# An encoder block on one core: where DRAM copies are issued, and which gate and up tiles use eight products

## The chip, the core and the metric

The kernel runs on one core of a Trainium2 chip. TensorE (PE) multiplies, VectorE (DVE), ScalarE (ACT) and GpSimd (POOL) do the elementwise work, and DMA engines move data between the device's memory (DRAM) and the on-chip memory, or within DRAM. Each engine has one queue and takes its instructions in order. DMAs are issued from the queues of SP (SyncE), ACT and POOL. The metric is the device time of one execution in microseconds (us); the median of several runs counts.

## What is computed

One layer, 512 tokens of width 1024, all in float32. From the reference, cut:

```python
h = rms_norm(x, norm_mix)
aq, ak, av, bq, bk, bv, ga, gb = split_cols(h @ w_in)
oa = gqa_attention(rope(rms_norm(aq)), rope(rms_norm(ak)), av)      # 8 heads of 64
ob = rms_norm(diff_attention(rope(bq), rope(bk), bv, lam), subln)   # 4 heads, two score maps each
y = sigmoid(ga) * (oa @ w_proj_a) + sigmoid(gb) * (ob @ w_proj_b)
x = x + y @ w_out
h = rms_norm(x, norm_ffn)
x = x + (silu(h @ w_gate) * (h @ w_up)) @ w_down                    # inner width 2816
return rms_norm(x, norm_final)
```

## The kernel before

**Precision.** Every float32 operand is split into a high part (a cast on ACT, `split_hi`) and a low part (the difference, on DVE, `split_lo`). A product is three matmuls, high by high, high by low, low by high (`mm3`, lines 92 to 94). `load_unit` (line 84) loads a weight unit of 128 x 1024 on SP's queue into a `raw` tile (three buffers) and splits it into `whi` and `wlo` (five buffers each).

**Stages.** First the projections of the first attention's heads (`group_a`) and of the first differential head (`group_b`). Then eight heads of the first attention (`attend_a`), with pieces of other work as fillers between heads. Then the four differential heads (`attend_b`), each woven with the projection of a later head or with gate columns (`gate_col`, products named gt). Then projections, output and the second norm. Last the channel mixer: gate and up in 22 tiles of 128 columns, and the down product.

**The differential heads.** For each of four token tiles `probs` makes two score maps (sc), their exponentials and reciprocals; POOL multiplies the first (p_b_..x, line 399), DVE combines both. The probabilities are transposed (ptp) and multiplied by the values (ob). Then the sums of squares pn go through POOL's power (rsb, line 112) into the matmuls pb (line 424).

**Sums of down weights.** The down product and gate and up use the seven products of a Strassen-like scheme. For the down product, sums and differences of weight blocks are formed in DRAM: tiles `td` of four kinds (td0 to td3), six pieces each. For each piece `tcopy` copies one block from `w_down` (line 453) and `tadd` adds a second one by an accumulating DMA (line 456). td1 adds td0's finished pieces, td3 those of td1. The list `tsums` runs through the kinds 0, 2, 1, 3; step k issues copy k and addition k - LAG, with LAG = 5. Copies and additions are all on POOL's queue. The steps stand in the four weaves with the differential heads, 8, 8, 7 and 6 of them.

**Gate and up.** Tiles 0 and 1 are computed as plain products by `ffn_in`, in two halves of 256 tokens: eight blocks of the inner width, twice (gate pg, up pu), three matmuls each. Tiles 2 to 21 use seven products of 256 columns (`g12`, `g5`, `g63`, `g7`, `g4`; q, p2 and r in the trace), 84 matmuls a tile. Their inputs come from `load_sums`: the raw unit, x (a load plus an accumulating load, lines 685 and 686), y (two DVE sums of x and raw, lines 694 and 695), each split; and from th and tl, sums of the hidden state, made on DVE after the norm with lowered priority. For tile 2 x and y take `raw` buffers (`early`).

**What sets the order.** The framework's scheduler orders each engine's queue by a simulated timeline; DMAs of `tsums` are kept in program order (`keep_in_program_order`). For every queue the order is fixed once the program is built.

Of the kernel before, what the change touches and what calls it, by code (L numbers as in the profile page):

```python
# [20 lines left out]
S = 512  # L21
# [5 lines left out]
NF = FF // P  # L27
# [2 lines left out]
LEFT_PAD = 48  # L30
RIGHT_PAD = 248
LATER = 400
LAG = 5


@with_exitstack
def kernel(
# [20 lines left out]
    nc = tc.nc  # L58
    v, a, g, pe = nc.vector, nc.scalar, nc.gpsimd, nc.tensor
# [312 lines left out]
    def attend_a(qT, kT, vt, fillers):  # L372
        for h in range(8):
            kv = h // 4
            if h >= 2:
                fillers[h - 2]()
            ps = []
            for tt in range(NT):
                nm = f"a{h}_{tt}"
                p_, r_ = probs(qT[h // 2][:, h % 2, :], kT[kv], tt, nm)  # L380
                g.tensor_scalar(out=p_, in0=p_, scalar1=r_, scalar2=1.0, op0=ALU.mult, op1=ALU.mult)  # L381
                ps.append(p_)
            av = ps_av.tile([P, S], F32, tag="av", name=f"oa_{h}")
            for kt in range(NT):
                ph, pl = transpose_p(ps, kt, f"a{h}_{kt}")
                pe.matmul(av, lhsT=vt[:, kt, kv, :], rhs=ph, start=kt == 0, stop=False)
                pe.matmul(av, lhsT=vt[:, kt, kv, :], rhs=pl, start=False, stop=kt == NT - 1)
            if h % 4 == 0:
                oA.append(u_tile(f"oA{kv}", F32))
            low = tmp.tile([HD, S], F32, tag="avt", bufs=1, name=f"low_{h}")  # L390
            a.copy(low, av[HD:P, :])
            v.tensor_tensor(out=oA[kv][HD * (h % 2):HD * (h % 2) + HD, h % 4 // 2, :], in0=av[0:HD, :], in1=low, op=ALU.add)
# [53 lines left out]
    tdram = [[dr.tile([P, 2, S], F32, name=f"td{i}_{p}") for p in range(NP)] for i in range(4)]  # L446
# [3 lines left out]
        return w_down[NU * j + 2 * p:NU * j + 2 * p + n, :, i * S:(i + 1) * S].rearrange("k p s -> p k s")  # L450

    def tcopy(i, p, src):
        return lambda: tc.keep_in_program_order(g.dma_start(tdram[i][p][:, :src.shape[1], :], src))

    def tadd(i, p, src):
        return lambda: tc.keep_in_program_order(g.dma_start(tdram[i][p][:, :src.shape[1], :], src, accum_op=ALU.add, max_dma_last_dim=4 * S))
# [7 lines left out]
    tsums = [tsum(i, p) for i in (0, 2, 1, 3) for p in range(NP)]  # L464
# [4 lines left out]
    def weave(*gens):  # L469
        gens = list(gens)  # L470
        while gens:
            for it in list(gens):
                if next(it, None) is None:
                    gens.remove(it)

    def steps(fs):
        for f in fs:
            f()
            yield True
# [8 lines left out]
        pe.matmul(pr[:, tt * P:(tt + 1) * P], lhsT=rstd[:, tt:tt + 1].to_broadcast([P, P]), rhs=ident, start=True, stop=True)  # L488
    a.copy(rstdB, pr)
    grp = [lambda: next(gen)]  # L490
    attend_a(*parts, grp * 3 + todo[:1] + grp + todo[1:2])
    weave(gen, steps(todo[2:4]))
    weave(attend_b(0, *nxt), group_b(2, nxt), steps(tsums[:8]))
    weave(attend_b(1, *nxt1), group_b(3, nxt1), steps(tsums[8:16]))
    weave(attend_b(2, *nxt), steps(todo[4:9]), steps(tsums[16:23]))
    weave(attend_b(3, *nxt1), steps(todo[9:13]), steps(tsums[23:]))
    for f in todo[13:]:
        f()
    attn.close()
# [151 lines left out]
    def bank(tag, nm, bufs=1):  # L651
        return ps_g.tile([P, S], F32, tag=tag, bufs=bufs, name=nm)
# [12 lines left out]
    def ffn_in(f, t0, t1, ug, uu):  # L665
        n = t1 - t0
        pg = bank("q", f"pg{f}_{t0}", 2)[:, :n]
        pu = bank("p2" if f else "r", f"pu{f}_{t0}")[:, :n]
        for acc, (hi, lo) in ((pg, ug), (pu, uu)):
            for kt in range(KT):  # L670
                c = slice(kt * P, (kt + 1) * P)
                mm3(acc, hi[:, c], lo[:, c], hh_[:, kt, t0:t1], hl_[:, kt, t0:t1], kt == 0, kt == KT - 1)
        t_ = (acts[f] if t0 else act_tile(f))[:, t0:t1]
        a.activation(t_, pg, AF.Sigmoid)
        v.tensor_tensor(out=t_, in0=pg, in1=t_, op=ALU.mult)
        v.tensor_tensor(out=t_, in0=pu, in1=t_, op=ALU.mult)
        if t0 == 0:
            act_parts(f)

    def load_sums(f):  # L680
        raw = wp.tile([P, UNIT], F32, tag="raw", bufs=3, name=f"raw_a{f}")
        nc.sync.dma_start(raw, w_gu[2 * f])
        early = f == 2
        x = wp.tile([P, UNIT], F32, tag="raw", bufs=3, name=f"x{f}") if early else tp_.tile([P, UNIT], F32, tag="x", bufs=3, name=f"x{f}")
        nc.sync.dma_start(x, w_x0[f])
        g.dma_start(x, w_x1[f], accum_op=ALU.add)  # L686
        r22 = tp_.tile([P, S], F32, tag="r22", bufs=3, name=f"r22_{f}")
        nc.sync.dma_start(r22, w_gu[2 * f + 1][:, S:])
        hi, lo = split_unit(raw, f"a{f}")
        w = wts[f] = {"11": (hi[:, :S], lo[:, :S]), "12": (hi[:, S:], lo[:, S:])}  # L690
        hi, lo = split_unit(x, f"x{f}")
        w["s1"], w["s3"] = (hi[:, :S], lo[:, :S]), (hi[:, S:], lo[:, S:])
        y = wp.tile([P, UNIT], F32, tag="raw", bufs=3, name=f"y{f}") if early else tp_.tile([P, UNIT], F32, tag="y", bufs=1, name=f"y{f}")
        v.tensor_tensor(out=y[:, :S], in0=x[:, :S], in1=raw[:, :S], op=ALU.add)
        v.tensor_tensor(out=y[:, S:], in0=y[:, :S], in1=raw[:, S:], op=ALU.add)
        hi, lo = split_unit(y, f"y{f}")
        w["s2"], w["s4"] = (hi[:, :S], lo[:, :S]), (hi[:, S:], lo[:, S:])
        h = sp_.tile([P, S], F32R, tag="h22", bufs=3, name=f"h22_{f}")
        l = sp_.tile([P, S], F32R, tag="l22", bufs=3, name=f"l22_{f}")
        split_hi(h, r22)  # L700
        split_lo(l, r22, h)
        w["22"] = (h, l)
# [17 lines left out]
    def g12(f):  # L720
        qb[f] = bank("q", f"q{f}", 2)[:, :H]
        p2 = bank("p2", f"p2_{f}")[:, :H]
        gprod(qb[f], f, "11", "11", True)
        gprod(p2, f, "12", "21", True, True)
        tg[f] = ft.tile([P, S], F32, tag="tg", name=f"tg{f}")
        a.copy(tg[f][:, :H], qb[f])
        v.tensor_tensor(out=tg[f][:, :H], in0=p2, in1=tg[f][:, :H], op=ALU.add)

    def g5(f):
        rb[f] = bank("r", f"r{f}")[:, :H]  # L730
        gprod(rb[f], f, "s1", "t1", True)
        p5c[f] = ft.tile([P, H], F32, tag="p5", name=f"p5_{f}")
        a.copy(p5c[f], rb[f])
# [78 lines left out]
    sums_a(0)  # L812
    p1 = [ps_d.tile([P, S], F32, tag="pd", name=f"p1_{b}") for b in range(2)]
    p2 = [ps_d.tile([P, S], F32, tag="pd", name=f"p2d_{b}") for b in range(2)]
    load_sums(2)
    g12(2)
    g5(2)
    for f in range(2, NF):
        if f + 1 < NF:
            load_sums(f + 1)  # L820
        g63(f)
        if f + 1 < NF:
            g12(f + 1)
        else:
            down0(NU - 2)
            pr_ = [bank("r", "pr_0"), bank("p2", "pr_1")]
        g7(f)
        if f + 1 < NF:
            g5(f + 1)
        else:  # L830
            product(0, 0, pr_, True, range(1))
        g4(f)
        if f % 2:
            sums_a(f // 2)
            if f + 1 < NF:
                down0(f // 2 - 1)
# [159 lines left out]
```

## Time and profile before

| | us |
|---|---|
| median of 3 runs | 761.25 (760.43 to 762.25) |
| profiled execution, whole time | 762.04 |
| profiled execution, span of the trace | 760.3 |
| TensorE busy in the span | 724.3 (95%) |
| VectorE busy | 553.0 (73%) |
| ScalarE busy | 423.8 (56%) |
| GpSimd busy | 193.9 (26%) |

Mean granted clock of TensorE 0.984 of full speed. All times in the trace are counted from the start of the span. A row of a timeline gives the start, the duration, the engine (SPq is the issuing queue of SP), the line, what is written and read without buffer numbers, and in brackets the idle time of the engine before it with what ended it. Durations of TensorE's matmuls overlap, so their pace is read from their starts.

### The profile page before, as it was taken

The page shows a single profiled execution, that of the slowest core. Times are in us where ns is not written, and L with a number is a line of the kernel's source. Part 1 is how long each engine was busy: PE and PEld are TensorE (multiplying, and loading weights), DVE is VectorE, ACT ScalarE, POOL GpSimd, SP SyncE. Part 2 cuts the span into 40 slices and gives each one's busy share as a digit, 9 for nine tenths or more (in the row PEclk, how much of TensorE's full clock was granted, in tenths as well). Part 3 has the DMA queues.
Part 4 walks back from the last instruction along what each step waited for, and adds up shares of the span by engine and source line. Part 5 has one row for each costly group of instructions (what it writes and reads, how often), then busy time and mean ns, then how long its engine had stood idle before and what let it go on. Part 6 is the DMA issues. An engine that isn't in the chain of part 4 may idle for free.

```text
span 760.3 us, 11984 instructions
## 1 busy us (share of the span) xinstructions
PE 724.3 (95%) x4407; PEld 651.0 (86%) x4407; DVE 553.0 (73%) x933; ACT 423.8 (56%) x765; POOL 193.9 (26%) x249
## 2 busy tenths in 40 slices
PE   5899999999999699899999999999999999999996
PEld 5789987789987588688888988999999999988885
DVE  5788698769876255458436779978887888877785
ACT  6356698867666366423226536555545555546672
POOL 3656443225774413010000021221221211110002
PEclk9899999999999889999999999999999999999999
DMA  8222212014999987514421289887777774459972
GB/s 316 82 65 75 57 45 81 8 41 137 274 300 282 298 193 156 187 52 137 139 83 48 64 251 293 243 225 236 218 208 224 200 194 158 146 172 332 320 270 110
DMA packets 46394, 131.52 MB, mean 173 GB/s; under 512 B 5664, under 2 KB 6560, under 8 KB 46336
## 3 DMA queue, kind: packets, MB, share of 16 engines
q1 hardware_dynamic: 29008, 84.55, 32.5%
q0 software_dynamic: 14736, 40.77, 23.3%
q10 hardware_dynamic: 2592, 5.45, 2.1%
q8 instruction: 34, 0.56, 0.3%
q14 instruction: 24, 0.20, 0.1%
HBM read 121.44 MB, written 32.37 MB: 202 GB/s over the span
## 4 chain that ended last, share of the span: by engine, by line
PE 75%; DMA 12%; DVE 5%; issue 3%; ACT 2%; POOL 2%; POOLq 0%; SPq 0%; ACTq 0%; DVEq 0%
DMA td<-in_w_down_dram 5%; PE q L92 5%; PE q L94 5%; PE q L93 5%; PE p L92 4%; PE p L93 4%; PE p L94 4%; DMA x<-in_w_x_dram 3%; PE r L94 2%; PE r L93 2%; PE r L92 2%; PE gt L92 2%; PE gt L93 2%; DMA td<-td 2%; PE gt L94 2%
## 5 line engine op out<-in xcount | busy, mean ns | idle before, releaser
L686 POOL DMA_DIRECT2D x<-in_w_x_dram x20 | 17.9, 894 | 130.2 <-DMA x<-in_w_x_dram 43.8
L93 PE MATMUL gt<-xgl,whi_g 128*128 128x512 f32 x128 | 51.0, 399 | 0.0
L92 PE MATMUL gt<-xgh,whi_g 128*128 128x512 f32 x128 | 51.0, 398 | 0.0
L94 PE MATMUL gt<-xgh,wlo_g 128*128 128x512 f32 x128 | 50.7, 396 | 0.0
L93 PE MATMUL acc_b<-wlo_b,xgh 128*128 128x384 f32 x128 | 43.6, 340 | 0.0
L92 PE MATMUL acc_b<-whi_b,xgh 128*128 128x384 f32 x128 | 43.4, 339 | 0.0
L94 PE MATMUL acc_b<-whi_b,xgl 128*128 128x384 f32 x128 | 43.4, 339 | 0.0
L763 POOL DMA_DIRECT2D sd<-s x44 | 28.8, 670 | 55.3 <-DVE s L760 25.3
L381 POOL TENSOR_SCALAR p_a<-p_a,r_a 128x512 f32<-128x512 f32 x32 | 23.7, 741 | 53.5 <-DVE r_a L359 46.0
L72 ACT CAST whi_y<-y 128x1024 fp32r<-128x1024 f32 x20 | 21.0, 1048 | 24.5 <-PE p2d L94 15.4
L79 DVE TENSOR_TENSOR wlo_y<-y,whi_y 128x1024 fp32r<-128x1024 f32 x20 | 24.4, 1222 | 10.0 <-ACT whi_y L72 10.0
L72 ACT CAST whi_a<-raw_a 128x1024 fp32r<-128x1024 f32 x20 | 21.0, 1048 | 16.6 <-issue 9.1
L79 DVE TENSOR_TENSOR wlo_t<-raw_t,whi_t 128x1024 fp32r<-128x1024 f32 (+1 forms) x24 | 27.0, 1130 | 3.2 <-ACT whi_t L72 3.0
L72 ACT CAST sh<-sr 128x512 fp32r<-128x512 f32 (+1 forms) x30 | 17.5, 583 | 21.1 <-PE p L93 8.0
L219 POOL TENSOR_TENSOR t_b<-z_b,csb 128x128 f32<-128x128 f32 x32 | 26.2, 947 | 11.7 <-ACT z_b L339 10.3
L94 PEld LDWEIGHTS gt<-xgh,wlo_g 128*128 128x128 f32 x128 | 24.4, 191 | 5.2
L93 PEld LDWEIGHTS gt<-xgl,whi_g 128*128 128x128 f32 x128 | 24.5, 191 | 4.9
L92 PEld LDWEIGHTS gt<-xgh,whi_g 128*128 128x128 f32 x128 | 24.3, 190 | 5.0
L92 PE MATMUL p<-whi_t,sh 128*128 128x512 f32 (+1 forms) x77 | 27.4, 360 | 1.0 <-DVE x L850 1.0
L357 ACT ACTIVATE p_a<-sc_a,nmax_a 128x512 f32<-128x512 f32 x32 | 22.4, 703 | 8.8 <-DVE nmax_a L354 7.9
L79 DVE TENSOR_TENSOR wlo_x<-x,whi_x 128x1024 fp32r<-128x1024 f32 x20 | 24.4, 1220 | 3.7 <-ACT whi_x L72 3.7
L93 PE MATMUL p<-wlo_t,sh 128*128 128x512 f32 (+1 forms) x77 | 26.9, 359 | 0.0
(391 smaller groups left out, 2815.1 us busy)
## 6 DMA issues: line engine op xcount, KB each, us to landing
td<-in_w_down_dram POOLq DMA_DIRECT2D x30, 512.0 KB, 16.9
raw_a<-in_w_gu_dram SPq DMA_DIRECT2D x20, 512.0 KB, 4.9
x<-in_w_x_dram SPq DMA_DIRECT2D x20, 512.0 KB, 4.9
x<-in_w_x_dram POOLq DMA_DIRECT2D x20, 512.0 KB, 6.7
raw_t<-td SPq DMA_DIRECT2D x20, 512.0 KB, 4.8
raw_g<-in_w_in_dram SPq DMA_DIRECT2D x16, 512.0 KB, 7.1
sr<-sd SPq DMA_DIRECT2D x25, 256.0 KB, 4.6
raw_b<-in_w_in_dram SPq DMA_DIRECT2D x16, 384.0 KB, 3.2
```

What stands on the lines that cost most here:

```text
L72: a.copy(dst, src)
L79: v.tensor_tensor(out=dst, in0=src, in1=hi.bitcast(F32), op=ALU.subtract)
L92: pe.matmul(acc, lhsT=lh, rhs=rh, start=start, stop=False, skip_group_check=loose)
L93: pe.matmul(acc, lhsT=lh, rhs=rl, start=False, stop=False, skip_group_check=loose)
L94: pe.matmul(acc, lhsT=ll, rhs=rh, start=False, stop=stop, skip_group_check=loose)
L219: g.tensor_tensor(out=t4[:, :, :, c], in0=q4[:, :, :, o], in1=bc(sin_, c), op=ALU.mult)
L357: a.activation(pr_, sc, AF.Exp, bias=nm_, scale=1.0, accum_out=s_)
L381: g.tensor_scalar(out=p_, in0=p_, scalar1=r_, scalar2=1.0, op0=ALU.mult, op1=ALU.mult)
L686: g.dma_start(x, w_x1[f], accum_op=ALU.add)
L763: g.dma_start(sdram[i][p][:, k, :], t)
```

## The change

- The copies of `tsums` are issued on SP's queue instead of POOL's, with LAG = 8 instead of 5. The first ten steps stand in the fillers of the first attention, two each from the second filler on; the rest follow in the weaves, 7, 7, 5 and 3.
- Tiles 2 and 3 of gate and up (up to NPLAIN = 4) are computed by `ffn_in`, over all 512 tokens at once: 48 matmuls of 512 columns a tile. The seven products begin at tile 4. PSUM banks for up alternate by even and odd tiles, and `early` is off.

```diff
-LAG = 5
+LAG = 8
+NPLAIN = 4
...
     def tcopy(i, p, src):
-        return lambda: tc.keep_in_program_order(g.dma_start(tdram[i][p][:, :src.shape[1], :], src))
+        return lambda: tc.keep_in_program_order(nc.sync.dma_start(tdram[i][p][:, :src.shape[1], :], src))
...
-    attend_a(*parts, grp * 3 + todo[:1] + grp + todo[1:2])
+    def also(f, more):
+        return lambda: [f()] + [m() for m in more]
+
+    fill = grp * 3 + todo[:1] + grp + todo[1:2]
+    attend_a(*parts, [also(f, tsums[2 * i - 2:2 * i] if i else []) for i, f in enumerate(fill)])
...
-    weave(attend_b(0, *nxt), group_b(2, nxt), steps(tsums[:8]))
+    weave(attend_b(0, *nxt), group_b(2, nxt), steps(tsums[10:17]))
...
-        pu = bank("p2" if f else "r", f"pu{f}_{t0}")[:, :n]
+        pu = bank("p2" if f % 2 else "r", f"pu{f}_{t0}")[:, :n]
...
-        early = f == 2
+        early = False
...
-    load_sums(2)
-    g12(2)
-    g5(2)
-    for f in range(2, NF):
+    for f in range(2, NPLAIN):
+        ffn_in(f, 0, S, load_unit(w_gu[2 * f], f"fg{f}"), load_unit(w_gu[2 * f + 1], f"fu{f}"))
+        if f % 2:
+            sums_a(f // 2)
+            down0(f // 2 - 1)
+    load_sums(NPLAIN)
+    g12(NPLAIN)
+    g5(NPLAIN)
+    for f in range(NPLAIN, NF):
```

POOL's queue ahead of rsb of the second differential head (rsb_1), before. p_b2_3x is the last multiply of the third head, td1_2 the third piece of kind 1:

```order
L399 TENSOR_SCALAR p_b2_3x_3017<-p_b2_3x_3017,r_b2_3x_3020 128x512
L453 DMA td3_1_237<-in_w_down_dram 256x1x512
L456 DMA td1_2_226<-td0_2_220 256x512
L453 DMA td3_2_238<-in_w_down_dram 256x1x512
L456 DMA td1_3_227<-td0_3_221 256x512
L453 DMA td3_3_239<-in_w_down_dram 256x1x512
L456 DMA td1_4_228<-td0_4_222 256x512
L453 DMA td3_4_240<-in_w_down_dram 256x1x512
L456 DMA td1_5_229<-td0_5_223 128x512
L112 TENSOR_TENSOR rsb_1_2826<-ms_2827,mhalf_73 128x4
```

The same place now:

```order
L457 DMA td1_3_227<-td0_3_221 256x512
L400 TENSOR_SCALAR p_b2_0x_2854<-p_b2_0x_2854,r_b2_0x_2857 128x512
L457 DMA td1_4_228<-td0_4_222 256x512
L400 TENSOR_SCALAR p_b2_1x_2912<-p_b2_1x_2912,r_b2_1x_2915 128x512
L457 DMA td1_5_229<-td0_5_223 128x512
L400 TENSOR_SCALAR p_b2_2x_2969<-p_b2_2x_2969,r_b2_2x_2972 128x512
L457 DMA td3_0_236<-td1_0_224 256x512
L400 TENSOR_SCALAR p_b2_3x_3027<-p_b2_3x_3027,r_b2_3x_3030 128x512
L457 DMA td3_1_237<-td1_1_225 256x512
L457 DMA td3_2_238<-td1_2_226 256x512
L113 TENSOR_TENSOR rsb_1_2839<-ms_2840,mhalf_73 128x4
```

Eight DMAs stood between the last multiply and rsb; now two additions do, and the additions are three pieces further on in the list.

SP's queue between the last weight load of the fourth differential head (raw_b3_3) and the next gate weights, where the first of these rows and the last followed each other before:

```order
L85 DMA raw_b3_3_2482<-in_w_in_dram 128x768
L454 DMA td1_5_229<-in_w_down_dram 128x512
L454 DMA td3_0_236<-in_w_down_dram 256x1x512
L454 DMA td3_1_237<-in_w_down_dram 256x1x512
L454 DMA td3_2_238<-in_w_down_dram 256x1x512
L454 DMA td3_3_239<-in_w_down_dram 256x1x512
L454 DMA td3_4_240<-in_w_down_dram 256x1x512
L454 DMA td3_5_241<-in_w_down_dram 128x512
L85 DMA raw_g2_2874<-in_w_in_dram 128x1024
```

Seven copies have come in between. The other seventeen stand further ahead: ten between the loads of gate columns in the first attention, seven between raw_b2_3 and raw_b3_0.

TensorE's queue at the end of the fourth differential head (ob_3, sums pn_3, then the first matmuls of the projection, pp), before:

```order
L365 MATMUL ptp_b3_3_3447<-ident_64,p_b3_3x_3355 128x128
L92 MATMUL ob_3_3408<-ph_b3_3_3452,vb3_2473 128x512
L93 MATMUL ob_3_3408<-pl_b3_3_3453,vb3_2473 128x512
L94 MATMUL ob_3_3408<-ph_b3_3_3452,vb3_2473 128x512
L419 MATMUL pn_3_3462<-ones_71,sqb_3_3460 128x1 x4
L92 MATMUL pp0_0_3624<-oh_a_3596,whi_p0_3614 128x512
```

The same place now, from the last of ob_3 on; 15 more gate matmuls of column 15 stand where these three are:

```order
L95 MATMUL ob_3_3410<-ph_b3_3_3452,vb3_2488 128x512
L93 MATMUL gt_15_3548<-xgh_97,whi_g15_3544 128x512
L94 MATMUL gt_15_3548<-xgl_98,whi_g15_3544 128x512
L95 MATMUL gt_15_3548<-xgh_97,wlo_g15_3545 128x512
...
L420 MATMUL pn_3_3462<-ones_71,sqb_3_3460 128x1 x4
L93 MATMUL pp0_0_3624<-oh_a_3596,whi_p0_3614 128x512
```

The head's products have moved ahead of 18 gate matmuls.

VectorE's queue around the last parts of the hidden state (hl of xt3), before:

```order
L79 TENSOR_TENSOR hl_3956<-xt2_1_4293,hh_3955 128x4x128
L79 TENSOR_TENSOR wlo_a2_4663<-raw_a2_4655,whi_a2_4662 128x1024
L694 TENSOR_TENSOR y2_4670<-x2_4657,raw_a2_4655 128x512
L695 TENSOR_TENSOR y2_4670<-y2_4670,raw_a2_4655 128x512
L79 TENSOR_TENSOR hl_3956<-xt3_0_4310,hh_3955 128x4x128
L79 TENSOR_TENSOR hl_3956<-xt3_1_4318,hh_3955 128x4x128
L675 TENSOR_TENSOR act0_4466<-pg0_0_4416,act0_4466 128x256
```

The same place now:

```order
L80 TENSOR_TENSOR hl_3956<-xt2_1_4293,hh_3955 128x4x128
L80 TENSOR_TENSOR wlo_fg2_4658<-raw_fg2_4655,whi_fg2_4657 128x1024
L80 TENSOR_TENSOR hl_3956<-xt3_0_4310,hh_3955 128x4x128
L80 TENSOR_TENSOR hl_3956<-xt3_1_4318,hh_3955 128x4x128
L680 TENSOR_TENSOR act0_4466<-pg0_0_4416,act0_4466 128x256
```

The two sums for y of tile 2 are gone from ahead of hl; the split there is now that of tile 2's plain gate weights.

## Rows read from the trace of the kernel before

**Rows 1.** Stretches: length; busy PE, PEld, DVE, ACT, POOL; PE clock; DMA share; GB/s.

```profile
247.00:272.00 25.00, 17.84 (x82) 14.93 (x81) 7.25 (x12) 9.27 (x14) 8.98 (x12) 0.80 1.09 289
...
304.00:330.00 26.00, 23.35 (x107) 18.44 (x107) 11.90 (x16) 10.63 (x14) 1.92 (x1) 0.93 0.52 174
...
441.00:462.00 21.00, 17.48 (x135) 16.20 (x134) 15.48 (x29) 8.88 (x16) 5.99 (x9) 1.00 0.98 280
462.00:640.00 178.00, 178.00 (x1399) 174.06 (x1398) 149.52 (x245) 95.91 (x149) 35.56 (x55) 1.00 0.79 223
```

**Rows 2.** Timeline of TensorE from the wait for rsb on.

```profile
265.94 2.08 PE L424 MATMUL pb<-ident,rsb 128*128 128x128 f32 x8 [7.16 <-POOL rsb L112]
...
271.65 0.45 PE L93 MATMUL gt<-xgl,whi_g 128*128 128x512 f32 x1
```

**Rows 3.** Timeline of POOL: copies and additions, up to the late rsb.

```profile
188.88 1.92 POOL L453 DMA_DIRECT2D td<-in_w_down_dram  x3
...
260.04 0.71 POOL L453 DMA_DIRECT2D td<-in_w_down_dram  x1 [0.34 <-DMA td<-in_w_down_dram]
263.95 0.85 POOL L456 DMA_DIRECT2D td<-td  x1 [3.21 <-DMA td<-td]
264.52 1.36 POOL L112 TENSOR_TENSOR rsb<-ms,mhalf 128x4 f32<-128x4 f32 x1
```

**Rows 4.** Chain that ended last: start, us, what (a DMA from issue to landing).

```profile
246.76 16.91 DMA td<-td
```

**Rows 5.** DMA from 160 to 184 us: queue's packets, MB, share; issues, KB, median us.

```profile
q0 software_dynamic: 308, 1.13, 15.3%
...
td<-in_w_down_dram POOLq DMA_DIRECT2D x3, 512.0 KB, 4.0
```

**Rows 6.** Timelines: SP's issues of raw_b3_3 and raw_g2, TensorE's next gate matmul.

```profile
161.09 0.33 SPq L84 DMA_DIRECT2D raw_b<-in_w_in_dram  x1
...
184.10 0.33 SPq L84 DMA_DIRECT2D raw_g<-in_w_in_dram  x1
...
221.94 0.39 PE L94 MATMUL gt<-xgh,wlo_g 128*128 128x512 f32 x1
```

**Rows 7.** The same DMA view from 280 to 312 us.

```profile
q0 software_dynamic: 1271, 2.43, 45.6%
...
td<-td POOLq DMA_DIRECT2D x4, 512.0 KB, 5.7
```

**Rows 8.** Waits of VectorE from 185 to 330 us: total, times, longest.

```profile
DVE p_b_0x L403 <- POOL p_b_0x L399: 4.5, 1, 4.5
```

**Rows 9.** Waits of TensorE from 185 to 330 us.

```profile
PE ob L93 <- DVE pl_b L79: 1.4, 2, 1.2
PE pn L419 <- ACT sqb L416: 1.2, 1, 1.2
PE ob L92 <- ACT ph_b L72: 1.2, 2, 0.8
```

**Rows 10.** Timelines: TensorE's scores and POOL's multiply, last head, fourth tile.

```profile
289.52 0.62 PE L352 MATMUL sc_b_3x<-kTb,qTb 128*128 128x512 f32 x2
...
296.12 0.69 POOL L399 TENSOR_SCALAR p_b_3x<-p_b_3x,r_b_3x 128x512 f32<-128x512 f32 x1 [7.68 <-DVE r_b_3x L359]
```

**Rows 11.** Timeline of TensorE: starts of matmuls of 512 and of 256 columns.

```profile
413.93 0.39 PE L93 MATMUL po<-wlo_o,yh 128*128 128x512 f32 x1
...
414.38 0.28 PE L92 MATMUL pg<-hh,whi_fg 128*128 128x256 f32 x1
...
415.69 0.28 PE L94 MATMUL pg<-hh,wlo_fg 128*128 128x256 f32 x1
```

**Rows 12.** Waits of TensorE from 400 to 470 us, the two longest.

```profile
PE pg L92 <- DVE act L675: 1.1, 1, 1.1
PE r L92 <- ACT whi_x L72: 1.1, 1, 1.1
```

**Rows 13.** Timeline of VectorE where it waits for x of tile 2.

```profile
425.88 0.69 DVE L694 TENSOR_TENSOR y<-x,raw_a 128x512 f32<-128x512 f32 x1 [4.99 <-DMA x<-in_w_x_dram]
```

More of the change, by code (lines that the diff above doesn't have):

```diff
@@ L490 @@
     grp = [lambda: next(gen)]
-    attend_a(*parts, grp * 3 + todo[:1] + grp + todo[1:2])
+    def also(f, more):
+        return lambda: [f()] + [m() for m in more]
+    fill = grp * 3 + todo[:1] + grp + todo[1:2]
+    attend_a(*parts, [also(f, tsums[2 * i - 2:2 * i] if i else []) for i, f in enumerate(fill)])
     weave(gen, steps(todo[2:4]))
-    weave(attend_b(0, *nxt), group_b(2, nxt), steps(tsums[:8]))
-    weave(attend_b(1, *nxt1), group_b(3, nxt1), steps(tsums[8:16]))
-    weave(attend_b(2, *nxt), steps(todo[4:9]), steps(tsums[16:23]))
-    weave(attend_b(3, *nxt1), steps(todo[9:13]), steps(tsums[23:]))
+    weave(attend_b(0, *nxt), group_b(2, nxt), steps(tsums[10:17]))
+    weave(attend_b(1, *nxt1), group_b(3, nxt1), steps(tsums[17:24]))
+    weave(attend_b(2, *nxt), steps(todo[4:9]), steps(tsums[24:29]))
+    weave(attend_b(3, *nxt1), steps(todo[9:13]), steps(tsums[29:]))
     for f in todo[13:]:
```

## The prediction

> **What bounds the kernel now.** I first read the table by stage [rows 1]. TensorE sets the pace: from 462 to 640 us it is busy for all 178 us at the full granted clock. Its losses sit in three places, and the changed lines touch all three. From 247 to 272 us it is busy 17.84 of 25 us, at a mean granted clock of 0.80. From 304 to 330 us it is busy 23.35 of 26 us, at 0.93. From 441 to 462 us it is busy 17.48 of 21 us.
>
> Then I read what it waits for. At 265.94 us TensorE has idled 7.16 us for POOL's rsb, the four reciprocal roots of the second differential head; its next matmuls stand 0.21 us apart for 128 columns until 271.65 us [rows 2]. POOL is late because it is held in its own queue: rsb stands right behind an addition that starts only at 263.95 us, after a wait of 3.21 us [rows 3]. The chain shows what ended that wait: the landing of an addition issued at 246.76 us, 16.91 us in flight [rows 4]. That one adds to another tile than the one issued at 263.95 us; it is the eighth DMA before it in POOL's queue (eight stand from 246.76 to 260.04 us, the waiting one not counted). So POOL is held by a count of eight DMAs in flight, while copies and additions together overfill the DMA engines: their share is 1.09 in this stretch [rows 1].
>
> **The copies, step by step.** Removed from POOL: 24 copies. Three issued alone took 15.3% of a 24 us stretch on POOL's queue [rows 5], 3.7 us or 1.2 us of all engines for each; the 24 (20 of full size, four of half) are worth 22 x 1.2 = 27 us of DMA time. They are not saved, they move: on SP's queue the first seventeen stand ahead of raw_b3_3, which was issued at 161.09 us, and the last seven (two of them halves, so six full ones) between it and raw_g2, issued at 184.10 us [rows 6]. Both stamps are set by buffers, not by SP, so I expect all copies landed by about 161 + 0.4 + 6 x 1.2 + 4 = 173 us; the last 4 is a lone copy's time to landing [rows 5]. Before, nearly all of them ran after 188 us, in the crowded stretch.
>
> The additions stay on POOL. How long they take without copies between is not shown, so I bound it. Below: four and a half issued from 280 us on, with the tail of an earlier one, filled 45.6% of 32 us, 14.6 us, so about 3 us of engine time each. Above: 5.7 us from issue to landing, one after the other [rows 7]. I take 4.5, nearer the upper end since each in that row had little company. The last addition ahead of rsb is that onto td3_2; it needs the landing of the fifteenth addition, onto td1_2, and every other landing that POOL waits for is older. Five additions go out singly before 184 us: two ahead of the last head of the first attention, three in the places that three copies had [rows 5]. The next ten, from 189 us on [rows 3], hold two halves, so they end at 189 + 9 x 4.5 = 230 us, or at 240 us with 5.7. POOL wants to issue td3_2 about 1 us after the issue of 246.76 us, at 248 us. So rsb leaves on time: **-7.16 us** of wait. The half clock after it goes too: the matmuls from 265.94 to 271.65 us (twelve of 128 columns, seven of 512) would take 12 x 0.11 + 7 x 0.227 = 2.9 us at full clock instead of 5.7, **-2.8 us**. What is late next: the pb matmuls, which read rsb, now stand 21 gate matmuls (21 x 0.227 = 4.8 us) behind the sums pn that rsb is made from; rsb itself takes 1.4 us [rows 3], so this holds.
>
> The same queue delays the head's probabilities. DVE waited 4.5 us for POOL's p_b_0x [rows 8], and TensorE 1.2 us for pl_b and 0.35 us for ph_b near 235 us [rows 9] (the longest of the first row, and what the last row has beside its longest). Between 0 and 1.5 us; I take **-1.2 us**, since POOL was free except for these waits.
>
> At the end of the attention TensorE waits 0.8 + 0.2 + 1.2 us for the last head [rows 9], and runs about 3.6 us at half clock (0.07 x 26 us, doubled) [rows 1], 1.8 lost: 4.0 us together. In the new order 18 gate matmuls stand between the last head's product ob and its sums pn, where none stood; they cover 18 x 0.227 = 4.1 us. But the same move pulls that head's fourth tile closer to its transposes: from its scores on, 26 gate matmuls, four of scores and eleven short ones lie between, 26 x 0.227 + 4 x 0.227 + 11 x 0.11 = 8.0 us. In this trace POOL's multiply of that tile came 6.6 us after its scores (289.52 to 296.12 us) and took 0.7 us [rows 10]; DVE's combination, about as long, still follows. That is 8.0 us too. So between -4.0 us and, with a new wait of some 2 us and half clock behind it, 0; I take **-2.8 us**, nearer the first since by these rows the two are even.
>
> Two additions enter POOL's queue in the first attention, about 0.9 us each [rows 3]. They stand ahead of the last head's multiplies; **+0.3 us**, between 0 and 1.8. The copies in that time meet DMA engines that are nearly idle, and the loads behind them are needed tens of us later (below).
>
> Here a rule speaks against the change. The trace shows POOL held by landings, not by issuing [rows 3, 4]. The Trainium skill (DMA: Bandwidth & Descriptors, section Issuing engines are not separate DMA queues) says that DMAs of all issuers share the same 16 engines and another issuer saves only issue time. By that sentence alone the 27 us of copies would crowd the additions as before and the 10 us would stay; it holds if the copies stay at the same time, and here they move by tens of us.
>
> **Tiles 2 and 3 in eight products.** Removed: for each tile 84 matmuls of 256 columns, added 48 of 512. Eleven steps of the first kind take 1.31 us, 0.119 each; two of the second 0.45 us, 0.225 each [rows 11]. So 2 x (48 x 0.225 - 84 x 0.119) = **+1.6 us** on TensorE, all of it on the path.
>
> What it buys is the start. Of the 21 us from 441 to 462 us, 135 matmuls account for 135 x 0.12 = 16.2 us, so up to 4.8 us are lost; by marked waits it is 3.5 us (21 - 17.48) [rows 1]. These waits name casts and differences of x and y [rows 12], which start only when the accumulating load of x has landed. Besides, DVE stood 4.99 us, until 425.88 us, for the x of tile 2 [rows 13], ahead of the last hl and the product that frees a PSUM bank, and TensorE waited 1.1 us for that product [rows 12]. In the new order no y stands there, and tile 4's x, y and splits have the 21.6 us of two plain tiles to arrive. Their weights come as plain loads with one split each; whi and wlo have five buffers, and fu2 and fg3 get theirs when the first half tiles are through, some us ahead of use. Gain between 4.6 and 5.9 us; I take 5.5, since the next thing late would be x of tile 5, and leave 0.3 for it: **-5.2 + 1.6 = -3.6 us**.
>
> **The sum.** -7.2 - 2.8 - 1.2 - 2.8 + 0.3 - 3.6 = -17.3 us. The profiled execution took 762.04 us (span 760.3, 1.7 around it), which gives 744.7; the median of the three runs is 0.8 us lower, so **744 us**. Its own ends, from the bounds above: 741 with every gain at its largest, 750 with every one at its smallest.
>
> **Rivals.**
> (a) *The additions alone are still too slow.* For it: their time in flight was 5.7 us even at the end [rows 7]; at over 6.5 us each the one onto td1_2 lands after 248 us and POOL stands again ahead of rsb. Against: the engines lose 27 us of copies. A rest of 4 us in place of 7.16, with half clock after it, gives back 5 to 7 us, and all of the wait 10: 749 to 754. The latter is what the rule on issuers would make of it.
> (b) *The wait moves to the last head.* The 8.0 us from scores to transposes are no more than that chain took [rows 10], and DVE has less idle time to be early in; with 2 to 4 us of wait and half clock behind it the term of -2.8 turns into 0 to +3: 747 to 750.
> (c) *Tile 4 starts as badly as tile 2 did*, because x of tiles 4 to 6 and the weights bunch on SP's queue: the 5.2 us stay and 1.6 are paid: 749 to 750.
> (d) *Slower than before: loads stuck behind copies in SP's queue.* Place: seven copies between raw_b3_3 and raw_g2. Issues are 23 us apart [rows 6], and the load's first possible use on TensorE is at 221.94 us [rows 6], 38 us after issue, of which some 8 are landing and split. The seven are worth six full ones: TensorE begins to wait when one takes over (23 + 30) / 6 = 9 us of the queue, and the gain of 17 us is eaten over (53 + 17) / 6 = 12 us; at 14 us a copy it is 774. Against: 1.2 us of engine time, and 4.0 us alone [rows 5]. The Trainium skill (DMA: Bandwidth & Descriptors, section Queues, rings and completion order) states the mechanism: descriptors of one ring are taken in order, while different rings alternate by packets, so before the change the loads could overtake the copies and now they can't.
> That the change does not do what it says is excluded by the order: the copies stand on SP, additions alone on POOL, tiles 2 and 3 under pg and pu.
>
> **Chances.** Forecast (740 to 748) 0.60; (a) 0.14; (b) 0.12; (c) 0.08; (d) 0.04; no change 0.02. A measurement of this kernel tells 0.2%, about 1.5 us, from none. (a) to (c) are all faster: faster 0.94, within 0.2% 0.02, slower 0.04. The range takes in (a) to (c) and the lower end with a us to spare: **739 to 754**.
>
> **What would show it.** Right: no wait of TensorE for rsb of the second head; POOL without waits for DMAs of td; the copies landed before 180 us, a DMA share clearly under 1 from 228 to 272 us, the granted clock at 1.00 there; no wait of TensorE from 440 to 470 us, plain tiles 0.225 us a matmul. Wrong: a wait for rsb or for p_b_3x of the last head; gate matmuls waiting for raw_g; casts of x or y named again, now at tile 4.

## The result and the profile after

The changed kernel takes 741.12 us (median of four runs, 740.41 to 741.17); the kernel before, on the same chip, 760.84 us (four runs, 758.63 to 762.25). The ratio is 0.9741, with a 95% interval from 0.9716 to 0.9766. The forecast was 744 us, range 739 to 754. The profiled execution has a span of 739.3 us in place of 760.3 us, so 21.0 us are to be found in the trace.

The first two lines are those of the page after on busy time and on the chain that ended last:

```profile
PE 717.8 (97%) x4335; PEld 644.3 (87%) x4335; DVE 545.3 (74%) x917; ACT 420.0 (57%) x755; POOL 174.3 (24%) x223
...
PE 92%; DMA 3%; DVE 2%; ACT 1%; issue 1%; SPq 0%; POOL 0%; POOLq 0%; ACTq 0%; DVEq 0%
```

TensorE is busy for 97% of the span and makes up 92% of the chain. The stretches of [rows 1] in the changed kernel, with the start of gate and up, which begins 16.5 us earlier, in two stretches (cut at 433.5 us, where tile 3 begins) (length; busy PE, PEld, DVE, ACT, POOL; PE clock; DMA share; GB/s):

```profile
247.00:272.00 25.00, 25.00 (x126) 20.78 (x125) 13.90 (x23) 17.58 (x25) 4.02 (x5) 1.00 0.57 128
304.00:330.00 26.00, 26.00 (x124) 21.76 (x123) 14.25 (x19) 10.02 (x12) 1.92 (x1) 1.00 0.41 142
397.84:433.50 35.66, 35.66 (x258) 33.76 (x256) 29.11 (x41) 19.13 (x31) 5.14 (x8) 1.00 0.58 182
433.50:462.00 28.50, 28.50 (x186) 26.16 (x185) 20.45 (x31) 12.59 (x19) 5.40 (x8) 1.00 0.86 249
```

All four are full, at the full granted clock. Between 150 and 480 us the view of waits has no entry for TensorE: its waits of [rows 2, 9, 12] are gone, as is VectorE's for p_b_0x [rows 8], and nothing has taken their place.

POOL's queue at the place of [rows 3], and TensorE's matmuls that read rsb [rows 2]:

```profile
244.19 1.79 POOL L457 DMA_DIRECT2D td<-td  x2
246.89 1.03 POOL L113 TENSOR_TENSOR rsb<-ms,mhalf 128x4 f32<-128x4 f32 x1 [0.91 <-DVE ms L112]
```

```profile
251.75 0.72 PE L425 MATMUL pb<-ident,rsb 128*128 128x128 f32 x5
```

POOL now waits for the numbers that rsb is made from (0.91 us, for ms), and not for a landing. rsb is done 3.8 us ahead of its reader; before, TensorE stood 7.16 us for it.

DMA from 160 to 184 us (queue's packets, MB, share; issues, KB, median us to landing), for [rows 5]; then from 185 to 247 us, for [rows 7]:

```profile
q1 hardware_dynamic: 1792, 3.54, 47.3%
...
td<-in_w_down_dram SPq DMA_DIRECT2D x5, 512.0 KB, 8.0
```

```profile
q0 software_dynamic: 3736, 7.16, 67.0%
...
td<-td POOLq DMA_DIRECT2D x8, 512.0 KB, 9.6
td<-in_w_down_dram POOLq DMA_DIRECT2D x5, 512.0 KB, 12.0
```

SP's queue (q1) took 47.3% of 24 us, 11.4 us, for seven copies worth six full ones and one weight load (1.1 us, the 4.6% of q1 in the same 24 us before): 1.7 us a copy, where I had taken 1.2 from POOL's queue. The difference is not one of the queues: of the three copies in [rows 5] the last was issued at 182.07 us and ran mostly after the window's end, as the 1.13 MB there show (three are 1.57 MB). The two that lie wholly within 168.5 to 181.5 us, in the kernel before, alone on POOL's queue, took 25.3% of 13 us, 1.6 us each:

```profile
q0 software_dynamic: 288, 1.05, 25.3%
...
td<-in_w_down_dram POOLq DMA_DIRECT2D x2, 512.0 KB, 4.0
```

So the 22 copies are worth some 36 us of DMA time and not 27. After the change the seven land 0.5 to 2.9 us apart, the last at 175.8 us; I had said 173. The additions alone (q0) took 67.0% of 62 us, 41.5 us, for thirteen full ones and three halves: **about 3 us each** (2.9 by the issues, 3.0 by the 7.16 MB). I had taken 4.5, between 3 and 5.7.

SP's queue at the place of [rows 6], and ACT's cast of the load behind the copies:

```profile
161.53 0.33 SPq L85 DMA_DIRECT2D raw_b<-in_w_in_dram  x1
161.91 4.83 SPq L454 DMA_DIRECT2D td<-in_w_down_dram  x7
184.56 4.19 SPq L85 DMA_DIRECT2D raw_g<-in_w_in_dram  x3
```

```profile
190.67 1.06 ACT L73 CAST whi_g<-raw_g 128x1024 fp32r<-128x1024 f32 x1 [2.79 <-DMA raw_g<-in_w_in_dram]
```

The copies did not hold the issue of raw_g2 (184.56 us after, 184.10 before). It took 6.1 us to land, before 4.5. ACT casts that load 22.8 us ahead of its first product and stood 2.79 us for it. That product is the 33rd of its kind (eight such a gate column, and this is the fifth column):

```profile
213.51 0.39 PE L93 MATMUL gt<-xgh,whi_g 128*128 128x512 f32 x1
```

In this run ACT's wait cost TensorE nothing; the experiments come back to it.

### The profile page after: what moved, and what is told of

The parts are those of the page before. It is cut to its first block, busy times and chain, and to the rows that moved or that the text cites. A ratio compares the mean times of both kernels' runs of the same rounds, so it can differ in the third digit from the quotient of the medians.

```text
span 739.3 us, 11815 instructions
## 1 busy us (share of the span) xinstructions
PE 717.8 (97%) x4335; PEld 644.3 (87%) x4335; DVE 545.3 (74%) x917; ACT 420.0 (57%) x755; POOL 174.3 (24%) x223
## 4 chain that ended last, share of the span: by engine, by line
PE 92%; DMA 3%; DVE 2%; ACT 1%; issue 1%; SPq 0%; POOL 0%; POOLq 0%; ACTq 0%; DVEq 0%
PE q L95 5%; PE q L94 5%; PE q L93 5%; PE gt L94 4%; PE gt L93 4%; PE gt L95 4%; PE p L95 4%; PE p L93 4%; PE p L94 4%; PE acc_b L93 3%; PE acc_b L94 3%; PE acc_b L95 3%; PE r L94 2%; PE r L93 2%; PE r L95 2%; PE pp L93 2%
## 5 line engine op out<-in xcount | busy, mean ns | idle before, releaser
L691 POOL DMA_DIRECT2D x<-in_w_x_dram x18 | 16.2, 899 | 126.5 <-DMA x<-in_w_x_dram 53.9
L73 ACT CAST whi_a<-raw_a 128x1024 fp32r<-128x1024 f32 x18 | 18.9, 1050 | 21.1 <-issue 11.7
L73 ACT CAST whi_y<-y 128x1024 fp32r<-128x1024 f32 x18 | 18.9, 1050 | 19.1 <-PE p2d L95 15.4
L80 DVE TENSOR_TENSOR wlo_y<-y,whi_y 128x1024 fp32r<-128x1024 f32 x18 | 22.0, 1221 | 8.7 <-ACT whi_y L73 8.7
L220 POOL TENSOR_TENSOR t_b<-z_b,csb 128x128 f32<-128x128 f32 x32 | 23.8, 763 | 11.6 <-ACT z_b L340 10.1
L95 PE MATMUL p<-whi_t,sl 128*128 128x512 f32 (+1 forms) x77 | 26.1, 360 | 0.1
```

Source lines behind the costliest of these rows:

```text
L73: a.copy(dst, src)
L80: v.tensor_tensor(out=dst, in0=src, in1=hi.bitcast(F32), op=ALU.subtract)
L95: pe.matmul(acc, lhsT=ll, rhs=rh, start=False, stop=stop, skip_group_check=loose)
L220: g.tensor_tensor(out=t4[:, :, :, c], in0=q4[:, :, :, o], in1=bc(sin_, c), op=ALU.mult)
```

## The experiments

My theory after the result: two independent gains. In the attention POOL's queue was held by landings, and whatever frees rsb from that gives back some 16 us; at gate and up the plain tiles remove the waits of the start. What was open: whether the queue (SP in place of POOL), the earlier time, or the greater distance did it, and whether the full DMA engines as such cost anything.

| run | median us | ratio to before (95%) |
|---|---|---|
| e1_copies_only | 747.05 | 0.9791 (0.9763 to 0.9819) |
| e2_plain_only | 756.92 | 0.9941 (0.9922 to 0.9961) |
| e3_pool_early | 742.67 | 0.9749 (0.9725 to 0.9773) |
| e4_sp_late | 746.96 | 0.9800 (0.9776 to 0.9825) |
| e5_lag5 | 741.03 | 0.9729 (0.9703 to 0.9755) |
| e11_lag8_late | 761.76 | 1.0008 (0.9993 to 1.0023) |
| e12_rsb_on_dve | 745.98 | 0.9801 (0.9775 to 0.9828) |
| e6_nplain3 | 741.54 | 0.9738 (0.9712 to 0.9763) |
| e7_nplain6 | 744.00 | 0.9763 (0.9738 to 0.9788) |
| e16_nplain3_early | 740.39 | 0.9716 (0.9689 to 0.9743) |
| e14_copies_x3 | 769.25 | 1.0088 (1.0059 to 1.0118) |
| e15_copies_x5 | 841.23 | 1.1038 (1.1009 to 1.1066) |

### Each part alone

```diff
-NPLAIN = 4
+NPLAIN = 2
...
-        early = False
+        early = f == 2
```

> The copies and additions of the changed kernel (SP's queue, from the first attention on, eight steps behind), but tiles 2 and 3 in seven products as before. The order of the attention on TensorE is that of the changed kernel, row by row. My theory: the two parts of the change are independent, so the whole gain in the attention is here. In the profiles TensorE reaches the first gate and up matmul 16.5 us earlier after the change (397.84 against 414.38 us), and the rest is 4.4 us shorter. So 761 - 16.5 = about 744.5 to 745.5 us, no wait of TensorE for rsb, and the waits near the start of tile 2 (4.6 us together before) still there. Rival: the parts meet on SP's queue or on VectorE at the start of gate and up, so that without the plain tiles some of the 16.5 us is lost again there: over 747 us.

The other half is the changed kernel with `LAG = 5`, the copies on POOL and the weaves and fillers of before:

> Only tiles 2 and 3 in eight products; copies on POOL's queue, five steps behind, in their old places. The attention's order on TensorE is that of the kernel before. My theory: 4.4 us off (the start of the seven products without its 4.6 us of waits and about 1 us of slow pace, against 1.4 us more TensorE work), so 756 to 757 us, with the wait of 7.2 us for rsb as before. Rival: part of what the changed kernel gains at the start of gate and up comes from the calmer DMA queues that the copies left behind; then this one gains 2 us or less, 759 us or more.

Copies alone give 15.1 us (762.15 us was before's median on that chip), plain tiles alone 5.2; together 20.3, and the whole change gave 19.7. Within their intervals the parts add up. TensorE's waits without plain tiles (total, times, longest), then those without moved copies:

```profile
PE pg L93 <- DVE act L680: 1.3, 1, 1.3
PE r L95 <- DVE wlo_x L80: 0.9, 1, 0.9
PE q L93 <- ACT tg L731: 0.9, 1, 0.9
```

```profile
PE pb L425 <- POOL rsb L113: 8.0, 1, 8.0
PE pn L420 <- ACT sqb L417: 1.2, 1, 1.2
```

Each half keeps, in the main, the waits that the other takes away.

### When, and from where

Copies back on POOL, all else as changed (`g.dma_start` in `tcopy`):

> The changed kernel with its copies back on POOL's queue: same early places, eight steps behind, plain tiles 2 and 3. It tells when from where. Theory 'time' (the copies are out of the way because they run while the DMA engines are half idle, whoever issues them): 741 to 744 us, no wait of TensorE for rsb; a copy costs POOL about 0.7 us of issue, which fits between its multiplies. Theory 'queue' (a copy on POOL takes one of the eight places in flight, and that alone held POOL): POOL waits again for landings of td and TensorE for rsb or for the probabilities, 747 to 757 us.

Copies on SP with before's weaves, fillers and `LAG = 5`, plain tiles kept:

> The changed kernel with copies on SP's queue but in their old places and five steps behind; plain tiles 2 and 3. SP has nothing to wait for at a copy, so it runs ahead: from the order I expect the first eight copies right behind the loads for the third head (about 121 us), the next eight behind those for the fourth (161 us), the last eight between gate loads from 184 us on, some 25 us later than in the changed kernel but most of them still ahead of the crowded stretch. Theory 'queue': POOL holds only additions, rsb leaves on time, 743 to 748 us (what the old order loses at the end of the attention, up to 4 us, may stay). Theory 'time': the last eight copies and the additions crowd one another, TensorE waits 3 us or more for rsb, 750 to 757 us.

e3 is as fast as the change to within 1.6 us. So it is not that copies left POOL. Its stretches from 228 us on, and what POOL waited for from 185 to 330 us:

```profile
228.00:247.00 19.00, 19.00 (x97) 15.82 (x96) 13.16 (x29) 13.16 (x26) 7.24 (x10) 1.00 1.09 256
247.00:272.00 25.00, 25.00 (x129) 20.77 (x127) 13.21 (x23) 17.23 (x26) 5.11 (x6) 1.00 0.71 167
```

```profile
POOL td L457 <- DMA td<-in_w_down_dram: 5.6, 2, 3.8
...
POOL td L457 <- DMA td<-td: 1.8, 1, 1.8
```

The DMA engines are as full as before up to 247 us (1.09), and POOL still stands for landings, 7.4 us in the three longest waits. But the list ends earlier, so these waits come at 204 to 234 us, where TensorE has cover, and none is open when rsb of the second head is due; two waits of TensorE with 0.9 us in all are the difference of the spans (740.2 against 739.3 us). Theory "time" held. The Trainium skill (DMA: Bandwidth & Descriptors, section Issuing engines are not separate DMA queues) says that DMAs share the 16 engines whoever issues them and another issuer saves only issue time; here the runs agree (ratio 0.9749 with the copies on POOL, 0.9741 with them on SP).

e4 lands at 747 us, within its range for "queue". POOL has no wait for a landing of td from 185 to 330 us, though the DMA engines are full:

```profile
228.00:247.00 19.00, 18.18 (x95) 14.90 (x94) 14.04 (x30) 13.31 (x27) 4.91 (x9) 1.00 1.10 250
```

But nothing holds SP at a copy, so it issued sixteen of the copies by 167 us all the same: on SP a later place in the list is hardly a later time. So e3 shows that leaving POOL's queue is not needed; whether it is enough with all copies late, no run tells. What remains of TensorE's waits are the two of the old order at the end of the attention (pn and pp) and one at 238.65 us, in the second head (ob):

```profile
PE pn L420 <- ACT sqb L417: 1.3, 1, 1.3
PE ob L93 <- ACT ph_b L73: 0.8, 1, 0.8
PE pp L94 <- DVE ol_a L80: 0.5, 1, 0.5
```

### The distance

The change with `LAG = 5`, then the kernel before with `LAG = 8` and nothing else:

> The changed kernel with LAG = 5 instead of 8, all else as changed; TensorE's order is the same row by row. The distance of additions from copies decides only what POOL may have to wait for. If the early copies carry the gain (theory 'time'), five steps do as well: 741 to 742 us, no wait of TensorE for rsb. Rival: with five steps the additions go out earlier, bunch ahead of rsb of the second head, and some of its wait of 7.2 us comes back: 744 us or more.

> The kernel before with LAG = 8 and nothing else: copies and additions on POOL, in the old places, seven products from tile 2 on. Three additions fewer stand ahead of rsb of the second head (the last is that onto td1_2 instead of td1_5), while all its copies stay. Theory 'work ahead of rsb' (what counts is how much DMA work of both kinds must be done before rsb may leave): three additions of 3 to 4 us are 9 to 12 us of DMA time, more than the 7.2 us of wait, so the wait goes or shrinks under 2 us and 748 to 753 us come out. Theory 'copies': as long as copies and additions share the crowded stretch and POOL's eight places, POOL stays late; the wait stays over 5 us and the time at 757 to 762 us.

The distance does nothing, at either place. My second expectation failed: I had reckoned that three additions fewer ahead of rsb would free it by 9 us. rsb left at the same time (264.91 us, against 264.52), and TensorE waited longer:

```profile
185.00:228.00 43.00, 43.00 (x250) 39.06 (x249) 34.37 (x74) 27.40 (x68) 29.30 (x36) 1.00 0.88 257
```

```profile
PE pb L424 <- POOL rsb L112: 8.9, 1, 8.9
```

The DMA share of this stretch was 1.02 before. Additions that go out later leave the engines idle first: 0.14 x 43 = 6 us of the 9 that I had counted as taken off the list.

### rsb out of POOL's queue, copies untouched

```diff
-        rsqrt_mean(rs, pn[:, 0:NT], P, NT)
+        ms = small.tile([P, 8], F32, tag="ms", name="ms")
+        v.tensor_scalar(out=ms[:, :NT], in0=pn[:, 0:NT], scalar1=1.0 / P, scalar2=EPS, op0=ALU.mult, op1=ALU.add)
+        v.reciprocal(out=rs, in_=ms[:, :NT])
```

> The kernel before, but the four factors of each differential head are made on VectorE by a reciprocal instead of POOL's power; this leaves out the square root in the heads' norm. Copies and additions are untouched. It tells whether POOL's queue, and not the DMA work itself, is the price. Theory: the wait of 7.2 us and about 3.8 us of half clock go, nothing else changes before the next head, whose own multiplies have 21 gate matmuls of cover: 750 to 752 us. Rival: the wait only moves, since the next head's multiplies on POOL stand in the same held queue: a wait of 3 us or more for them, 754 to 761 us.

This is the run that tells most. It leaves out the square root in the heads' norm, so it is there to measure and replaces nothing. The kernel before, with all its copies and additions on POOL at the old time, gains 14.4 us, within the intervals as much as the moved copies alone (e1). Its stretch around the old wait, and POOL's waits from 185 to 330 us:

```profile
247.00:272.00 25.00, 25.00 (x127) 20.80 (x126) 14.31 (x26) 16.99 (x25) 9.77 (x13) 1.00 1.08 294
```

```profile
POOL td L458 <- DMA td<-in_w_down_dram: 16.6, 8, 3.5
...
POOL td L458 <- DMA td<-td: 7.2, 3, 3.1
```

The DMA engines are full (1.08), POOL stands 23.8 us for landings ahead of additions (20.8 before), and TensorE loses nothing at the full clock. So neither the crowd nor POOL's standing was the price, but one instruction of 1.4 us that TensorE needs and that was queued behind it. I had expected 750 to 752 us; the rest is the end of the attention, which the framework laid out in the changed kernel's order here too (the last head's products 18 gate matmuls ahead of its sums).

### The number of plain tiles

`NPLAIN` set to 3, to 6, and to 3 with `early = f == NPLAIN`:

> The changed kernel with one plain tile less (tile 2 in eight products, seven products from tile 3 on). By the profile of the changed kernel a plain tile costs 48 x 0.224 = 10.8 us, one in seven products 84 x 0.120 = 10.1 us, so 0.7 us less: 740.4 us, if one plain tile is cover enough for the loads, x and y of tile 3. Rival: it is not; waits for x and y of tile 3 come back, 1 to 4 us of them, 742 to 744 us.

> The changed kernel with tiles 2 to 5 in eight products. It prices a plain tile beside the seven products in steady state. By the changed kernel's profile: 48 x 0.2243 - 84 x 0.120 = 0.69 us a tile, so 1.4 us more, 742.5 us. Rival: tiles 4 and 5 still paid something for the start of the seven products, then less than 0.5 us more, 741.6 us or below.

> One plain tile (tile 2), seven products from tile 3 on, and x and y of tile 3 in buffers of the weights' ring, so that x need not wait for memory that the hidden state's sums still held until 419 us in the run with one plain tile; there TensorE waited 0.94 us for x. If that wait goes: 740.5 us. Rival: x and y now wait for the ring's buffers behind the plain tile's weights, 742 us or more.

With one plain tile a wait of 0.9 us appears at tile 3 (the first line; TensorE's waits from 400 to 480 us, and the same with x and y in the weights' buffers), so what the tile saves is lost. With early buffers 0.3 us is left. From the first gate matmul to the last landing of the output these runs took 341.7 and 341.5 us, against 340.4 in the changed kernel, where I had reckoned with 0.7 less; the marked waits do not cover that, and the rest is open. By their intervals neither is told apart from the changed kernel, and neither is e5.

```profile
PE r L93 <- DVE act L681: 0.9, 1, 0.9
```

```profile
PE r L93 <- DVE tg L744: 0.3, 1, 0.3
```

With two tiles more the same stretch grew by 1.2 us (341.6 against 340.4 us), near the 1.4 expected. The run is 2.9 us longer all the same: POOL's closing drain at the end of the program took 6.7 us, against 3.2 to 3.5 us in all other profiles. No run tells why.

### The price of SP's queue

```diff
-        return lambda: tc.keep_in_program_order(nc.sync.dma_start(tdram[i][p][:, :src.shape[1], :], src))
+        def issue():
+            for d in (spare[i][p], spare[4 + i][p], tdram[i][p]):
+                r = tc.keep_in_program_order(nc.sync.dma_start(d[:, :src.shape[1], :], src))
+            return r
+        return issue
```

> The changed kernel with each copy on SP issued three times, twice into spare DRAM tiles that nobody reads. It prices the queue of SP (my rival on loads stuck behind copies). In the changed kernel copies landed 1.3 to 1.8 us apart, so a place of the list costs the ring 3 x 1.5 = 4.5 us here. Seven places stand between the last load for the fourth head (issued at 161.5 us) and the next gate weights, used on TensorE at 220.4 us: worth six full ones, 27 us, they land near 195 us. So no wait of TensorE for a load, rsb on time, 741 to 743 us. Rival: the loads are late earlier than I reckon, or the copies' extra DMA work (48 x 1.2 us of engine time, mostly from 70 to 190 us) holds the additions and with them rsb: 746 us or more.

> The same with each copy issued five times, 7.5 us of SP's ring for a place. Between raw_b3_3 and the next gate weights 6 x 7.5 = 45 us: these land near 210 us, still ahead of 220 us. But the first ten places stand ahead of gate weights that TensorE used at 114.7 and 143.6 us in the changed kernel: eight places from 71 us on are 60 us, so the second of these loads lands near 135 to 140 us, ten places and the third near 150 us, after its use. Theory (ring in order, 1.5 us a copy): TensorE waits about 5 us or more for gate weights in the first attention, and everything behind is late: 746 us or more, with raw loads named. Rival: DMAs of one queue overlap enough that loads pass, no wait for a load: 741 to 744 us.

The first expectation was wrong by 27 us; of its rival the first reason held. The chain of e14 (start, us, what), ACT's cast and TensorE's wait:

```profile
201.52 22.75 DMA raw_g<-in_w_in_dram
```

```profile
224.30 1.04 ACT L73 CAST whi_g<-raw_g 128x1024 fp32r<-128x1024 f32 x1 [20.22 <-DMA raw_g<-in_w_in_dram]
```

```profile
226.61 0.49 PE L254 MATMUL pt_b<-identr,qs_b 128*128 128x128 f32 x2 [17.75 <-ACT kTb L256]
```

Two steps of my sum failed. The copies between 165.8 us and the load, worth eighteen full ones, took 3.1 us each, not 1.5, because most of them ran beside the additions. From 179 to 222.5 us:

```profile
q0 software_dynamic: 2260, 4.35, 59.1%
q1 hardware_dynamic: 3400, 6.87, 47.1%
```

SP's queue had under half of the DMA engines' time, and a copy took of it what it takes elsewhere: 20.5 us for 6.87 MB is 1.6 us for each 512 KB. And TensorE did not wait for the weights: ACT did, with the cast, which stands in ACT's queue some 20 us ahead of the product (22.8 in the changed kernel). Everything ACT owed TensorE (the keys kTb) stood behind it. With five copies a place loads are late three times, and TensorE waits 6.1, 29.7 and 35.0 us, now for the casts themselves; the kernel takes 100 us more than the changed one. The longest waits are

```profile
PE gt L93 <- ACT whi_g L73: 42.8, 3, 35.0
PE acc_b L93 <- ACT whi_b L73: 29.7, 1, 29.7
```

The Trainium skill (DMA: Bandwidth & Descriptors, section Queues, rings and completion order) has descriptors of one ring taken in order; the load that waited 22.75 us behind copies agrees with it. That is half of the load's delay against the changed kernel: it also went out 17.0 us later (201.52 against 184.56 us), since SP's later issues in e14 stand at landings and not at the 0.6 us that an issue takes.

## Why the prediction was right, and where its sizes were off

The direction, the three places and the order of the terms held; the gain was 19.7 us by the medians and 21.0 in the profiled runs, where I had 17.3. It is the lower one of the forecast's own ends, every gain at its largest.

| term | forecast us | trace us |
|---|---|---|
| wait for rsb and half clock behind it | -7.2, -2.8 | -7.2, -2.8 |
| the head's probabilities | -1.2 | -1.5 |
| end of the attention | -2.8 | -4.4 |
| two additions on POOL in the first attention | +0.3 | 0 |
| drains ahead of waits in the attention | not counted | -1.1 |
| tiles 2 and 3, gate and up | -3.6 | -4.4 |
| before 160 us | 0 | +0.5 |
| sum | -17.3 | -20.9 |

The trace's column is what the kernel before shows as lost there and the changed kernel no longer shows; the 2.8, some 1.8 of the 4.4 at the end of the attention (both half clock) and the drains are estimates from its rows. The attention as a whole (from the first scores of the differential heads to the first gate matmul) is 17.0 us shorter, and its terms add up to that.

**The wait for rsb.** Right as worked out, and the cover too: the last addition ahead of it was issued at 244.8 us (I had 248), and rsb was ready 3.8 us early. The 4.5 us for an addition was too much; at about 3 rival (a) had no ground. The 1.2 us for a copy was too little, by the reading of [rows 5] above; it set the time of 173 us for the last landing, and with 1.65 the same sum gives 175.3, but no term of the gain. The count of eight DMAs is borne out: in the kernel before, e3, e11 and e12 POOL's waits of 0.3 us or more for landings of td (13, 4, 12 and 16 of them) all end 0.3 us after the landing of the eighth DMA before. Whether the chip or the framework sets the eight, no run tells.

But the reason I gave was wider than the cause. I wrote of copies and additions that overfill the engines; e12 shows that with the engines as full as ever only the place of rsb behind POOL's waits had a price, and e3 that it is enough to start early, on either queue. That the share would be "clearly under 1 from 228 to 272 us" was half wrong: it is 0.96 from 228 to 247 us, and that did no harm.

**Probabilities and the end of the attention.** The whole of both went, where I took 1.2 of 1.5 and 2.8 of 4.0; at the end a wait of 0.4 us that I had not counted went too (TensorE for ol_a, at 323.75 us before).

```profile
PE pp L93 <- DVE ol_a L79: 0.4, 1, 0.4
```

At the end I had called the new order even: 8.0 us of cover for the fourth tile against a chain of 8.0. The cover was 8.1 us, and the chain took 7.4, since POOL's multiply came 5.9 us behind the scores (before 6.6 [rows 10]):

```profile
278.83 0.63 PE L353 MATMUL sc_b_3x<-kTb,qTb 128*128 128x512 f32 x2
...
286.94 0.27 PE L366 MATMUL ptp_b<-ident,p_b_3x 128*128 128x128 f32 x1
```

```profile
284.69 0.69 POOL L400 TENSOR_SCALAR p_b_3x<-p_b_3x,r_b_3x 128x512 f32<-128x512 f32 x1 [4.96 <-DVE r_b_3x L360]
```

By 0.7 us rival (b) did not happen. That also is close; e4 prices the old order: its waits at the end of the attention are 1.8 us, with the one of 0.8 in the second head 2.6, and the spans differ by 2.9 us (742.2 against 739.3). The profiled run is e4's fastest; by the ratios it is 4.5 us.

**Drains.** This step was missing. Idle time is counted from a matmul's end, but a matmul of 512 columns in a row gives way after 0.23 us and takes 0.39 to its end [rows 11]. So by estimate each wait costs some 0.16 us more than it shows: seven waits in the attention 1.1 us, and about as much among the seven at the start of gate and up.

**Gate and up.** The price of the plain tiles was right: the two took 21.79 us (below), 10.9 each, against 84 x 0.119 = 10.0, so 1.8 us where I had 1.6; e7 has 1.2 for two more. From the first gate matmul (414.38 us before [rows 11], 397.84 after) to the end of the span it was 345.9 us and is 341.5, 4.4 less; so the start gave back 6.2 us, more than my upper bound of 5.9: the marked waits there were 4.6 us and the drains are 1.1, the last half microsecond I cannot place. I had held 0.3 back for tile 5, which had no wait. Rival (c) is excluded by the absence of waits.

```profile
422.59:444.38 21.79, 21.79 (x99) 18.02 (x97) 14.69 (x25) 7.15 (x10) 6.07 (x9) 1.00 1.03 319
```

**Rival (d), loads stuck behind copies.** It did not happen, but it was much nearer than I wrote. I let TensorE's first use, 38 us after the issue, set the slack, and found 9 us of the queue for a copy before anything waits. e14 gave each place 56.6 / 6 = 9.4 us, and by that rule TensorE would have waited 6 x 0.4 = 2.4 us; it waited 17.75, and the kernel was slower than before. Two readings failed. The matmul at 221.94 us [rows 6] belongs to the next column: the first product with this load was at 213.40 us before, 29 us after the issue, which leaves (23 + 21) / 6 = 7.3 us for a copy and gives 56.6 - 44 = 12.6 us of wait. And the reader that counts is not TensorE but ACT's cast, which stood 2.79 us already in the changed kernel and holds what ACT owes TensorE behind it.

**The first 160 us.** TensorE reached the first differential head 0.5 us later than before (160.56 against 160.10 us). A wait of 1.4 us at 16.6 us (0.2 before) is the only difference there that I found, and the change does not touch that place; e1 has no such wait and e3, e12 and e14 have 0.9 to 1.1 us of it.

## What to carry to other kernels

When an engine both issues DMAs and computes, look at which of its results the bottleneck needs, and what its queue holds ahead of them: taking that one instruction off the queue, or starting the DMAs early enough, was worth as much as moving all the traffic. For a load that is to queue behind others, the deadline is its first reader on any engine, not its first use in a product, since an in-order engine stops for it with all else that it owes. And a wait on the bottleneck costs its idle time, the drain ahead of it and, where the granted clock fell, the half clock behind it: count all three. (After the wait of 7.16 us the clock was 0.50 of full speed for 5.7 us; e4's waits of 0.5 to 1.3 us left it at 1.00.)

## What was not expected of the hardware

- A 512 KB copy within DRAM took 1.6 to 1.7 us of the DMA engines, alone on POOL's queue, on SP's, and beside additions in e14, where they landed 3.1 us apart. An accumulating one took about 3 us.
- Some kernels with a rest of waits vary more from run to run: copies alone 742.9 to 747.9 us in five, at a mean granted clock of 0.988 to 0.995; the changed kernel 740.4 to 741.2 us in four, at 0.992 to 0.994. Why is open, since one run of each has a profile.
- POOL's closing drain took 6.7 us in e7 and 3.2 to 3.5 us in all other profiles; open.
